# Four conditioning vectors of the attention layer: from TensorE steps to scaled sums on GpSimd and ScalarE

## The chip, the cores and the metric

The kernel runs on one core of one Trainium2 chip. The time is the device time of one execution in microseconds (us). The engines are named as in the profile: PE is TensorE's matmuls and PEld its weight loads, DVE is VectorE, ACT ScalarE, POOL GpSimd, SP SyncE; a "q" behind a name (SPq) is the part of an engine that issues transfers.

## What is computed

A backbone of two layers on 512 latent tokens and 256 context tokens of width 1024. Layer 0 mixes tokens by a Fourier transform and a short convolution, layer 1 by windowed attention with 16 query heads and 4 key heads; each layer ends in a mixture of 32 experts. Every layer has six conditioning vectors per sample, made by one product with a large matrix:

```python
mod_l = (silu(c) @ w_mod[layer] + b_mod[layer])[:, None, :]     # c: (1, 1024), w_mod[layer]: (1024, 6144)
mod_c = silu(c_ctx) @ w_mod[layer] + b_mod[layer]
sh1_l, sc1_l, g1_l, sh2_l, sc2_l, g2_l = split(mod_l, 6, axis=-1)
hl = modulate(rms_norm(xl, norm_mix_g[layer]), sh1_l, sc1_l)
...
yl, yc = window_attention(hl, hc, ...)                          # layer 1: softmax(q k + sink) v, then @ w_o
xl = xl + g1_l * yl
hl2 = modulate(rms_norm(xl, norm_ffn_g[layer]), sh2_l, sc2_l)
xl = xl + g2_l * hier_moe(hl2, ...)                             # last layer: latent tokens alone
```

In layer 1, the last, the context's part of the last four vectors (gate g1, shift sh2, scale sc2, gate g2) is not needed.

## The kernel before

**Conditioning.** A `ModFeed` makes two vectors (a group, 2048 columns) in four steps. A step has 2 MB of `w_mod` (two of the eight slices of 128 rows, 2048 columns) in a shared slot and multiplies it by `sil`, the silu of both samples, on TensorE: 8 matmuls of 512 columns at line 1035, recorded as 16. In layer 1, for groups 1 and 2 (g1 to g2), VectorE adds each step's PSUM tile to `bm` (line 1040), where GpSimd's queue has put `b_mod` (line 1028); after a group's four steps GpSimd's queue stores the rows of `bm` to `mod_d` in memory (line 1043). SyncE loads the weights (line 1013). Of these eight steps two stand in the projection of Q, K and V and six behind attention blocks 1 to 6.

**Attention** works on eight blocks (two halves of the heads by four blocks of 128 queries). Round `n` of the loop computes the scores and the exponentials of block `n`, two heads in each of four parts `i` (score matmul line 1783; mask and maximum on VectorE, line 1787; exponential with its sum on ScalarE, line 1789), and turns the probabilities of block `n-1` into values: `pv_tile` transposes eight heads' probabilities on TensorE (line 1830) and copies them out of PSUM (line 1833; tiles of the second four heads with odd `t` on VectorE, all others on ScalarE), `pv_mm` multiplies by V into the one PSUM tile `O` (line 1845). `s_end` works out the reciprocal of the softmax denominator in `es` (lines 1810 to 1813). `pv_end` spreads it over the partitions by TensorE (line 1856), and scales: ScalarE copies the factors (1858), VectorE multiplies them with `O` into SBUF (1859), ScalarE rounds the result to `ohi` (1862), VectorE takes the rest, `olo` (1863).

**Projection by w_o** (`mixer_out`): the matrix comes in two halves of 512 columns, hf0 in slot 2 and hf1 in slot 1, by four transfers each of 64 partitions (line 1893). For each of eight row slices ScalarE rounds it (line 1344) and VectorE takes the rest (line 1345); a tile of 128 tokens takes 24 matmuls (line 1378). `router` loads two vectors as `md` (line 1325) and has 8 matmuls with it (line 1331) within the first token tile of hf0. Behind hf1 the experts' weights (line 721) stream through a ring of buffers, among them the two that hold the rounded w_o.

**Order.** The code is written in the order of the loops; a scheduler then fixes each engine's order ahead of time. Every engine, SyncE's queue of transfers among them, works through its own list in order, so an instruction that waits holds all behind it. The buffers of a pool decide when a transfer may start: slot 1 holds the copied probabilities (`av`), slot 2 the conditioning weights.

Of the kernel before, what the change touches and what calls it, by code (L numbers as in the profile page):

```python
# [10 lines left out]
F32 = mybir.dt.float32  # L11
# [3 lines left out]
AF = mybir.ActivationFunctionType  # L15
# [5 lines left out]
D = 1024  # L21
# [64 lines left out]
def body(tc, I, out, upto=None, dbg=None):  # L86
# [57 lines left out]
    ones = one_.to_broadcast([128, 128])  # L144
    epst = stat.tile([128, 1], F32, name="epst")
    V.memset(epst, EPS)
    rsq = stat.tile([128, 2, 4], F32, name="rsq")

    def slot(i, shape, dt=F32):
# [22 lines left out]
    def rows_and_logits(m, xm, hq, a2, b2, ws, crow, route, h2dst, wk, psum):  # L172

        xv = xm.rearrange("t (p k) -> t k p", k=8)
        parts, last = isinstance(h2dst, list), m == route.NT - 1
        h2 = hq.tile([128, D], F32, name="h2", bufs=2 if parts else 3)
        ss = small.tile([128, 1], F32, name="ss")
        if last:

            s0 = small.tile([128, 1], F32, name="s0")  # L180
            r0 = small.tile([128, 1], F32, name="rb")
            S.activation(h2[:, 0:512], xm[:, 0:512], AF.Square, accum_out=s0)
            V.tensor_scalar(r0, s0, 1.0 / D, EPS, op0=ALU.mult, op1=ALU.add)
            if not parts:
                G.tensor_mul(h2[:, 0:512], xm[:, 0:512], a2[:, 0:512])
            yield
        hT = wk.tile([128, 8, 128], F32, name="hT")
        for hf in range(2):
            p = psum([128, 4, 128])
            for q in range(4):  # L190
                T.transpose(p[:, q, :], xv[:, hf * 4 + q, :], ident)
            S.copy(hT[:, hf * 4:hf * 4 + 4, :], p)
        if last:
# [803 lines left out]
    class ModFeed:  # L997
# [20 lines left out]
        def step(self, again=-1):  # L1018
# [22 lines left out]
            if q == 3:  # L1041
                for s in range(2):
                    G.dma_start(mod_d[l, s, g * 2048:(g + 1) * 2048].rearrange("(q n) -> q n", q=4), bm[s:128:32, :])


    xsrc = [I["x"][0, m * 128:(m + 1) * 128, :] for m in range(4)] + [I["ctx"][0, m * 128:(m + 1) * 128, :] for m in range(2)]
    pp = pool("ps0", space=PSUM)
# [535 lines left out]
    run(rest0)  # L1583

    feed = ModFeed([(1, 1), (1, 2)], lambda: cps([128, 512]), False)
    feed.load(0)
    close(mps, R1b, R1a, mp)
    pp = pool("ps1", space=PSUM)  # L1590
    kvp = pool("kvp")
# [3 lines left out]
    gqk = ro.tile([128, 2, 64], F32, name="gqk")  # L1595
    with tc.issue_after(near["done"].ins):
        rotary()
    cb = pool("cb")
    hpl = pool("hpl", side="right")

# [102 lines left out]
            S.copy(kS[part][0:64, :, ms], p)  # L1703
            (V.tensor_copy)(kS[part][64:128, :, ms], p)

    feed.psum_tile = lambda: psB([128, 512])
    raw0 = load_qkv(0, 3)
    for i in range(8):
        if i == 4:
            hc = slot(0, [128, 2, 8, LC], F32R)  # L1710
            hhi.append(hc[:, 0])
            hlo.append(hc[:, 1])
        for f, d in ((st_norm, 0), (st_kv, 1), (st_kt, 3)):
            if 0 <= i - d < (4 if f is st_kt else 6):
                f(i - d)
        if i == 0:
            feed.step()
        if i == 2:
            feed.step(None)
    close(cb)  # L1720

    qS = []
# [79 lines left out]

    ohi, olo = [hpl.tile([128, 8, L], F32R, name=n) for n in ("hhi", "hlo")]
    av = slot(1, [128, 8, 512])
    feed.load(2)
    def s_end(n):
        G_ = n // 4
        nm, ls = st_[n][1:3]
        es = small.tile([128, 8], F32, name="es")
        V.tensor_add(es, nm, sink[:, G_ * 8:G_ * 8 + 8])  # L1810
        S.activation(es, es, AF.Exp)
        V.tensor_add(es, es, ls)
        V.reciprocal(es, es)
        st_[n][3] = pp.tile([128, 512], F32, name="O", bufs=1)
        st_[n][4] = es

    pts = [0]

    def pv_tile(n, t):
        G_, b = divmod(n, 4)  # L1820
        Ps, po = st_[n][0], st_[n][3]
        kt = blk(b)[0]
        nk = len(kt)
        if t >= nk:
            return
        pt = []
        for gl in range(2):
            p = psB([128, 4, 128])
            for i in range(4):
                T.transpose(p[:, i, :], Ps[gl * 4 + i][:, t * 128:(t + 1) * 128], ident)  # L1830
            d = av[:, pts[0] % 4]
            pts[0] += 1
            (V.tensor_copy if gl and t % 2 else S.copy)(d, p.rearrange("p i q -> p (i q)"))  # L1833
            pt.append(d)
        st_[n].append(pt)

# [11 lines left out]
    def pv_end(n):  # L1848

        G_, b = divmod(n, 4)  # L1850
        po, es = st_[n][3:5]
        p = psB([128, 4, 128])
        for i in range(4):
            for gl in range(2):
                c = gl * 4 + i
                T.matmul(p[gl * 64:gl * 64 + 64, i, :], es[:, c:c + 1].to_broadcast([128, 64]), ident, start=True, stop=True)
        o = av[:, 4 + n % 2]
        S.copy(o, p.rearrange("p i q -> p (i q)"))
        V.tensor_mul(o, o, po)
        ov = o.rearrange("p (i q) -> p i q", i=4)  # L1860
        hs = ohi[:, G_ * 4:G_ * 4 + 4, b * 128:(b + 1) * 128]
        S.copy(hs, ov)
        V.tensor_sub(olo[:, G_ * 4:G_ * 4 + 4, b * 128:(b + 1) * 128], ov, hs.bitcast(F32))

    s_end(0)
    for n in range(1, 9):
        if n < 8:
            s_begin(n)
        for i in range(5):
            if n < 8 and i < 4:  # L1870
                s_head(n, 2 * i)
                s_head(n, 2 * i + 1)
            if n == 1 and i < 2:
                st_qt(1, 2 + i)
            if n > 0:
                pv_tile(n - 1, i)
                pv_mm(n - 1, i - 1)
        if n > 0:
            pv_mm(n - 1, 4)
            pv_end(n - 1)  # L1880
        if n < 7:
            feed.step()
        if n < 8:
            s_end(n)
    close(wp, ro, ap_, kvp, fdp)

    wov = I["w_o"][0].rearrange("(G gl i d) n -> gl d G i n", G=2, gl=2, i=4)

# [69 lines left out]
```

## Time and profile before

| | |
|---|---|
| time, median of 3 runs (lowest, highest) | 1679.38 us (1678.43, 1681.98) |
| profiled execution: its time, its span | 1680.04 us, 1678.1 us |
| busy: PE, DVE, ACT, POOL | 1557.0, 726.6, 441.8, 124.5 us |
| mean granted clock of TensorE, share of full | 0.967 |
| read from memory, mean rate | 499.31 MB, 301 GB/s |

The span runs from the first to the last instruction of one execution. The busy times are sums over stages with different limits, so a stage is read from its own stretch. Rows name a line of the kernel, an engine, an operation, and `out<-in` by the program's names; what stands in brackets at a row's end is how long the engine was idle just before, and what ended that.

### The profile page before, as it was taken

How to read it: one execution, taken by the hardware profiler on the slowest of the kernel's cores; microseconds unless marked ns; L12 is line 12 of the kernel's file. 1: busy time of each engine (PE TensorE's matmuls, PEld its weight loads, DVE VectorE, ACT ScalarE, POOL GpSimd, SP SyncE). 2: the span in 40 equal slices, each digit the busy share in tenths (PEclk: the TensorE clock that was granted, in tenths of full speed). 3: DMA queues.
4: the chain of work that ended last, by engine and by line, in shares of the span. 5: the costliest groups of instructions: out<-in, count | busy, mean ns of one | idle time of the engine just before them, and what ended most of it. 6: DMA issues, size and time to landing. Idle time of an engine off the chain costs nothing.

```text
span 1678.1 us, 21585 instructions
## 1 busy us (share of the span) xinstructions
PE 1557.0 (93%) x8123; PEld 869.8 (52%) x8123; DVE 726.6 (43%) x1638; ACT 441.8 (26%) x879; POOL 124.5 (7%) x128
## 2 busy tenths in 40 slices
PE   5999989889999999999889999999899999986787
PEld 3677878634444444444357765558444544531332
DVE  4432335963325443434468954545622322320213
ACT  5321212211111111111256665544221221210110
POOL 2510001300000000000212300000000000000000
PEclk8999989889999999999989999999899999999899
DMA  9775253789999999999811114253699999999996
GB/s 375 273 283 191 86 195 101 273 329 419 420 419 402 384 419 419 420 419 420 338 71 51 49 56 186 75 140 75 263 420 420 419 420 420 419 418 421 420 420 253
DMA packets 106398, 503.52 MB, mean 300 GB/s; under 512 B 18384, under 2 KB 33232, under 8 KB 52272
## 3 DMA queue, kind: packets, MB, share of 16 engines
q1 hardware_dynamic: 95776, 464.09, 69.9%
q0 software_dynamic: 7344, 34.81, 5.4%
q10 hardware_dynamic: 3168, 3.17, 0.6%
q8 instruction: 67, 1.10, 0.3%
q14 instruction: 43, 0.35, 0.1%
HBM read 499.31 MB, written 5.34 MB: 301 GB/s over the span
## 4 chain that ended last, share of the span: by engine, by line
PE 35%; DMA 10%; DVE 3%; ACT 2%; issue 1%; SPq 0%; DVEq 0%; ACTq 0%
PE p L860 8%; DMA w<-in_w_dram 5%; PE yp L931 5%; DMA hhi<-in_w_dram 3%; PE cp L809 3%; PE O L1845 3%; PE A L1378 3%; PE tp L765 3%; PE A L1660 2%; PE B L1830 2%; PE A L1783 2%; PE B L1035 1%; DMA r<-in_w_dram 1%; PE tp L772 1%; DMA w<-in_w_qkv_dram 1%
## 5 line engine op out<-in xcount | busy, mean ns | idle before, releaser
L860 PE MATMUL p<-w,xt 128*64 128x512 f32 (+1 forms) x1024 | 336.5, 611 | 16.6 <-DMA w<-in_w_dram 16.5
L860 PE MATMUL p<-r,xt 128*64 128x512 f32 (+1 forms) x784 | 284.5, 614 | 11.5 <-DMA r<-in_w_dram 11.0
L810 DVE TENSOR_TENSOR x<-x,cp 128x512 f32<-128x512 f32 x224 | 148.0, 685 | 96.6 <-PE cp L809 96.5
L809 PE MATMUL cp<-y,ot 128*128 128x512 f32 x616 | 173.6, 417 | 10.7 <-DVE x L810 6.9
L873 DVE TENSOR_TENSOR sg<-sg,p 128x512 f32<-128x512 f32 x29 | 20.0, 688 | 369.8 <-PE p L860 358.4
L860 PEld LDWEIGHTS p<-w,xt 128*64 128x64 f32 (+1 forms) x1024 | 100.2, 134 | 129.7 <-issue 98.2
L931 PE MATMUL yp<-w,ht 128*64 128x512 f32 (+1 forms) x512 | 162.7, 602 | 2.9 <-DMA w<-in_w_dram 2.9
L860 PEld LDWEIGHTS p<-r,xt 128*64 128x64 f32 (+1 forms) x784 | 84.3, 137 | 146.4 <-issue 122.6
L809 PEld LDWEIGHTS cp<-y,ot 128*128 128x128 f32 x616 | 106.8, 191 | 53.9 <-DVE x L810 28.3
L931 PE MATMUL yp<-r,ht 128*64 128x512 f32 (+1 forms) x368 | 131.6, 613 | 2.1 <-DMA r<-in_w_dram 1.4
L797 ACT CAST y<-yp 128x512 fp32r<-128x512 f32 x58 | 34.0, 586 | 280.7 <-DVE yp L793 185.5
L1378 PE MATMUL A<-r,r 128*128 128x512 f32 x288 | 72.9, 411 | 2.6 <-ACT r L1344 2.4
L931 PEld LDWEIGHTS yp<-r,ht 128*64 128x64 f32 (+1 forms) x368 | 38.5, 137 | 67.8 <-issue 63.7
L931 PEld LDWEIGHTS yp<-w,ht 128*64 128x64 f32 (+1 forms) x512 | 47.0, 132 | 47.0 <-issue 39.5
L860 PE MATMUL p<-hhi,xt 128*64 128x512 f32 (+1 forms) x128 | 62.6, 642 | 6.6 <-DMA hhi<-in_w_dram 6.6
L1787 DVE CUSTOM_DVE_ANT_0 A<-A,band,nsink 128x640 f32<-128x640 f32 (+1 forms) x56 | 46.5, 833 | 47.4 <-PE A L1783 36.4
L1378 PEld LDWEIGHTS A<-r,r 128*128 128x128 f32 x288 | 56.1, 198 | 14.9 <-ACT r L1344 2.7
L863 ACT ACTIVATE sg<-p 128x512 f32<-128x512 f32 x29 | 17.3, 597 | 157.4 <-PE p L860 157.4
L799 DVE TENSOR_TENSOR y<-yp,y 128x512 fp32r<-128x512 f32 x58 | 40.1, 692 | 40.3 <-ACT y L797 40.3
L1845 PE MATMUL O<-w,v 128*64 128x512 f32 x144 | 56.9, 615 | 0.6 <-ACT w L1833 0.6
L795 DVE SCALAR_TENSOR_TENSOR yp<-yp,gs,grow 128x512 f32<-128x512 f32 x26 | 19.7, 759 | 77.7 <-PE yp L931 77.7
L860 PE MATMUL p<-hlo,xt 128*64 128x512 f32 (+1 forms) x112 | 52.5, 618 | 0.0
(428 smaller groups left out, 2560.7 us busy)
## 6 DMA issues: line engine op xcount, KB each, us to landing
w<-in_w_dram SPq DMA_DIRECT2D x191, 1024.0 KB, 19.8
r<-in_w_dram SPq DMA_DIRECT2D x143, 1024.0 KB, 19.8
w<-in_w_mod_dram POOLq DMA_DIRECT2D x12, 2048.0 KB, 8.6
hhi<-in_w_dram SPq DMA_DIRECT2D x23, 1024.0 KB, 19.7
hlo<-in_w_dram SPq DMA_DIRECT2D x23, 1024.0 KB, 19.8
w<-in_w_mod_dram SPq DMA_DIRECT2D x11, 2048.0 KB, 8.8
w<-in_w_in_even_dram SPq DMA_DIRECT2D x13, 512.0 KB, 9.0
w<-in_w_out_even_dram SPq DMA_DIRECT2D x2, 2048.0 KB, 8.2
```

Source lines behind the costliest of these rows:

```text
L765: T.matmul(p, oh[:, m, :], near["h2"][m][i][:, hf * 512:hf * 512 + 512], start=n == 0, stop=n == 7)
L797: hi = S.copy(Yr[j, hf][0], ys)
L799: V.tensor_sub(Yr[j, hf][1], ys, Yr[j, hf][0].bitcast(F32))
L809: T.matmul(p, OT[j][:, m * 128:(m + 1) * 128], Yr[j, hf][i], start=n == 0 and i == 0, stop=n == len(js) - 1 and i == 1)
L810: return V.tensor_add(xs, xs, p)
L860: T.matmul(ps[rs], X[b][:, q, rs], W[j, wn, ab][:, q, :], start=q == 0, stop=q == 7)
L931: T.matmul(py_[hf][rs, :], HT[b][:, q % 4, rs], W[j, "w2", ab][:, q % 4, hf * 512:hf * 512 + 512], start=q % 4 == 0, stop=q % 4 == 3)
L1378: T.matmul(ps, lhs(m, a, j), whl[b][:, j, :], start=j == 0 and i == 0, stop=j == 7 and i == 2)
L1660: T.matmul(ps, h[st][:, k, ms], whl[k][b], start=k == 0 and i == 0, stop=k == 7 and i == 2)
L1783: T.matmul(ps[:, o0:o0 + w], qS[G_][:, c, b * 128:(b + 1) * 128], kS[part][:, 2 * G_ + c // 4, k0:k0 + w], start=part == 0, stop=part == 1)
L1787: V.tensor_tensor_reduce(out=ps[:, 0:w], in0=ps[:, 0:w], in1=bnd, op0=ALU.add, op1=ALU.min, scale=1.0, scalar=nsink[:, hd:hd + 1], accum_o ...
L1845: T.matmul(po[gl * 64:gl * 64 + 64, :], vts[kt[t]][:, (2 * G_ + gl) * 64:(2 * G_ + gl) * 64 + 64], pt[gl], start=t == 0, stop=t == nk - 1)
```

## The change

Vectors 2 to 5 of layer 1 are now made by a `SumFeed`, 16 steps of 1 MB (one vector, two row slices). In a step GpSimd multiplies the first slice by its 128 values of `sil` and ScalarE the second, and GpSimd adds them to a running sum of 128x1024. When the four steps of a vector are done, `finish` sums over the partitions by two matmuls with ones, VectorE adds `b_mod`, and SyncE stores the row. Only the latent sample is computed. The steps stand within the blocks, after parts `i` of rounds 1 to 7; finishes at the start of rounds 4, 6 and 7 and behind round 8. Slot 2 is cut in two rooms of 1 MB. With it: the two small additions of `s_end` go to GpSimd (`s_sum`, at part 2 of the next round), all copies for the second four heads go to VectorE, and `pv_end` multiplies within PSUM, so that `ohi` and `olo` are read from there.

```diff
+        def load(self):
+            if self.ld < len(self.todo):
+                v, q = self.todo[self.ld]
+                c = self.vectors[v] * D
+                Y.dma_start(self.room[self.ld % len(self.room)], I["w_mod"][self.layer].rearrange("(p k) n -> p k n", k=8)[:, 2 * q:2 * q + 2, c:c + D])
+                self.ld += 1
+
+        def step(self):
+            v, q = self.todo[self.cp]
+            w, acc = self.room[self.cp % len(self.room)], self.acc[v % 2]
+            self.cp += 1
+            for i in range(2):
+                t = w[:, i] if q + i else acc
+                if i:
+                    S.activation(t, w[:, i], AF.Copy, scale=sil[:, 2 * q + i, 0:1])
+                else:
+                    G.tensor_scalar(t, w[:, i], sil[:, 2 * q + i, 0:1], None, op0=ALU.mult)
+                if q + i:
+                    G.tensor_add(acc, acc, t)
+            self.load()
+
+        def finish(self, ps):
...
+            rows = bm[0:64:32, :]
+            Y.dma_start(rows, I["b_mod"][self.layer, c:c + D].rearrange("(q n) -> q n", q=2))
+            for cb in range(2):
+                T.matmul(ps[cb * 32:cb * 32 + 32, :], onef.to_broadcast([128, 32]), acc[:, cb * 512:cb * 512 + 512], start=True, stop=True)
+            V.tensor_add(bm[0:64], ps[0:64], bm[0:64])
+            Y.dma_start(mod_d[self.layer, 0, c:c + D].rearrange("(q n) -> q n", q=2), rows)
...
-        if i == 0:
-            feed.step()
-        if i == 2:
-            feed.step(None)
...
-    feed.load(2)
+    wm = slot(2, [128, 2, 2, D])
+    feed = SumFeed(1, (2, 3, 4, 5), [wm[:, 0], wm[:, 1]], acc)
...
+        G.tensor_add(es, nm, sink[:, G_ * 8:G_ * 8 + 8])
         S.activation(es, es, AF.Exp)
-        V.tensor_add(es, es, ls)
+        G.tensor_add(es, es, ls)
...
-            (V.tensor_copy if gl and t % 2 else S.copy)(d, p.rearrange("p i q -> p (i q)"))
+            (V.tensor_copy if gl else S.copy)(d, p.rearrange("p i q -> p (i q)"))
...
-        V.tensor_mul(o, o, po)
-        ov = o.rearrange("p (i q) -> p i q", i=4)
+        V.tensor_mul(po, po, o)
+        ov = po.rearrange("p (i q) -> p i q", i=4)
...
+            if i == 2:
+                s_sum(n - 1)
+            if i == 0 and n in (4, 6, 7):
+                feed.finish(psB([128, 512]))
+            if i in {1: (0, 2, 4), 4: (0, 2, 4), 8: ()}.get(n, (1, 3)):
+                feed.step()
...
+        if n == 8:
+            feed.finish(psB([128, 512]))
```

The lines of before that the text names move by some 40: the scores 1783 to 1822, the values 1845 to 1888, the rounding of w_o 1344 to 1389, its matmuls 1378 to 1423, its loads 1893 to 1940. New are 1061 (load), 1071 and 1073 (scaling on ScalarE and GpSimd), 1075 (addition), 1084 to 1088 (finish).

SyncE's list at the end of attention, before: `w_8410` is hf0 of w_o (slot 2), `w_8557` hf1 (slot 1), `w_8938` and `w_8939` experts' weights, `wr` to `gf` the router's.

```order
L1893 DMA w_8410<-in_w_o_dram 64x4x512 x4
L721 DMA w_8938<-in_w_dram 128x2048 x2
L1314 DMA wr<-in_w_router_g_dram 128x8x4
L1315 DMA wr<-in_w_router_e_dram 128x8x32
L1316 DMA br<-in_b_router_g_dram 128x4
L1317 DMA br<-in_b_router_e_dram 128x32
L1319 DMA gf<-in_norm_ffn_g_dram 128x8
L1337 DMA gr<-mod_d 128x512
L1325 DMA md_8433<-mod_d 128x2x8
L1337 DMA gr<-mod_d 128x512
L721 DMA w_8939<-in_w_dram 128x2048
L1893 DMA w_8557<-in_w_o_dram 64x4x512 x4
```

The same place now: `w_7074` is the sixteenth load of the conditioning weights, `w_8413` hf0 of w_o, `w_8560` hf1. The two halves of an expert's weights (here `w_8939`) stand just ahead of these rows.

```order
L1359 DMA wr<-in_w_router_g_dram 128x8x4
L1061 DMA w_7074<-in_w_mod_dram 128x2x1024
L1360 DMA wr<-in_w_router_e_dram 128x8x32
L1361 DMA br<-in_b_router_g_dram 128x4
L1362 DMA br<-in_b_router_e_dram 128x32
L1364 DMA gf<-in_norm_ffn_g_dram 128x8
L1382 DMA gr<-mod_d 128x512
L1940 DMA w_8560<-in_w_o_dram 64x4x512 x4
L1382 DMA gr<-mod_d 128x512
L1940 DMA w_8413<-in_w_o_dram 64x4x512 x4
L1088 DMA mod_d<-bm 2x512
L1370 DMA md_8436<-mod_d 128x2x8
```

The loads of hf0 have moved from ahead of the experts' weights to behind those of hf1, and the load of `md` behind them; the last load of the conditioning weights stands behind the router's first.

TensorE's list at the same place, before, from the last value matmuls into the projection (`r_8400` is the rounded w_o, `r_8401` its rest). The router's matmuls (line 1331) follow after 16 matmuls of line 1378.

```order
L1845 MATMUL O<-w_7094,v_5925 64x512 x2
L1856 MATMUL B<-cst,es 64x128 x8
L1845 MATMUL O<-w_7094,v_5926 64x512 x2
L1378 MATMUL A<-r_8400,hhi 128x512
L1378 MATMUL A<-r_8400,hlo 128x512
L1378 MATMUL A<-r_8400,hhi 128x512
L1378 MATMUL A<-r_8400,hlo 128x512
L1378 MATMUL A<-r_8401,hhi 128x512
```

The same place now (`acc_5913` is the running sum of the fourth vector, `r_8403` the rounded w_o).

```order
L1888 MATMUL O<-w_7073,v_5928 64x512 x2
L1899 MATMUL B<-cst,es 64x128 x8
L1888 MATMUL O<-w_7073,v_5929 64x512 x2
L1086 MATMUL B<-acc_5913,onef 32x512 x2
L1423 MATMUL A<-r_8403,hhi 128x512
L1423 MATMUL A<-r_8403,hlo 128x512
L1423 MATMUL A<-r_8403,hhi 128x512
L1423 MATMUL A<-r_8403,hlo 128x512
L1376 MATMUL B<-wr,md_8436 128x36 x8
```

The two matmuls of the last finish now stand between the last values and the projection, and the router's matmuls after 4 of the projection's matmuls instead of 16.

## Rows read from the trace of the kernel before

**Rows 1.** windows: busy us of PE, PEld, DVE, ACT, POOL, then granted clock, DMA share, GB/s
```profile
920.00:940.00 20.00, 19.08 (x96) 15.18 (x96) 19.12 (x43) 8.17 (x18) 6.56 (x5) 1.00 0.00 0
980.00:1000.00 20.00, 20.00 (x128) 11.29 (x124) 9.13 (x20) 10.60 (x23) 0.00 (x0) 1.00 0.28 106
```

**Rows 2.** groups of instructions in attention: count, busy us, mean ns, idle before
```profile
L1833 ACT COPY w<-B 128x512 f32<-128x512 f32 x56 | 32.6, 588 | 33.7 <-PE B L1830 30.0 <-PE O L1845 3.3
...
L1035 PE MATMUL B<-w,sil 128*32 128x512 f32 x96 | 16.1, 601 | 0.0
...
L1833 DVE COPY w<-B 128x512 f32<-128x512 f32 x16 | 11.0, 689 | 13.9 <-PE B L1830 13.9
```

**Rows 3.** timeline of TensorE around three feed steps: start, duration, name
```profile
854.35 3.60 PE L1035 MATMUL B<-w,sil 128*32 128x512 f32 x16 [2.67 <-ACT r L1556]
857.88 2.12 PE L1660 MATMUL A<-w,hhi 128*128 128x512 f32 x8
...
870.01 1.92 PE L1035 MATMUL B<-w,sil 128*32 128x512 f32 x16
871.87 1.16 PE L1552 MATMUL B<-cst,xn 128*128 128x128 f32 x8
...
1021.15 1.05 PE L1035 MATMUL B<-w,sil 128*32 128x512 f32 x4
1022.13 0.74 PE L1783 MATMUL A<-kS,w 128*128 128x256 f32 x4
```

**Rows 4.** two stretches at the first feed step, with the granted clock (PEclk)
```profile
856.00:858.00 2.00, 2.00 (x13) 0.32 (x6) 0.00 (x0) 1.83 (x6) 1.81 (x1) 0.56 0.00 0
858.00:860.00 2.00, 2.00 (x9) 1.64 (x10) 1.98 (x12) 0.00 (x0) 0.00 (x0) 1.00 0.53 94
```

**Rows 5.** GpSimd's groups: additions, scalings and casts
```profile
L201 POOL TENSOR_TENSOR h<-x,a 128x1024 f32<-128x1024 f32 x4 | 9.6, 2410 | 124.2 <-ACT h L199 124.2
...
L1148 POOL TENSOR_SCALAR xnl<-xnl,A,AB 128x512 f32<-128x512 f32 x3 | 3.3, 1106 | 0.0
...
L1515 POOL CAST w<-r 128x512 fp32r<-128x512 f32 x4 | 2.3, 604 | 0.0
```

**Rows 6.** ScalarE's operation on 128x1024
```profile
L1670 ACT ACTIVATE xn<-x,rq x4: 1134/1149/1152, 860.9 to 880.5; 128x1024 f32<-128x1024 f32 x4
```

**Rows 7.** SyncE's queue at the end of attention
```profile
1086.96 2.63 SPq L1893 DMA_DIRECT2D w<-in_w_o_dram  x4
1108.70 5.26 SPq L721 DMA_DIRECT2D w<-in_w_dram  x2
1114.06 0.58 SPq L1314 DMA_DIRECT2D wr<-in_w_router_g_dram  x1
```

**Rows 8.** timeline of TensorE from the last score matmul to the projection
```profile
1107.89 0.74 PE L1783 MATMUL A<-kS,w 128*128 128x256 f32 x4
...
1118.05 0.50 PE L1378 MATMUL A<-r,hhi 128*128 128x512 f32 x1 [0.34 <-ACT r L1344]
...
1119.99 0.62 PE L1378 MATMUL A<-r,hhi 128*128 128x512 f32 x2
...
1120.68 0.62 PE L1378 MATMUL A<-r,hhi 128*128 128x512 f32 x2
...
1123.89 1.94 PE L1331 MATMUL B<-wr,md 128*128 128x36 f32 x16 [1.67 <-issue]
```

**Rows 9.** the eight w_o loads, from issue to landing
```profile
DMA to landing us min/median/max: 5.7/8.5/11.2
```

**Rows 10.** DMA issues: count, KB each, median us to landing
```profile
r<-in_w_qkv_dram SPq DMA_DIRECT2D x2, 1024.0 KB, 6.8
...
md<-mod_d SPq DMA_DIRECT2D x3, 8.0 KB, 4.4
```

**Rows 11.** second w_o half's transfer, experts' stage: DMA share, GB/s
```profile
1132.00:1140.00 8.00, 8.00 (x37) 6.56 (x36) 2.57 (x4) 0.00 (x0) 0.00 (x0) 1.00 1.04 208
1300.00:1600.00 300.00, 269.02 (x1366) 116.28 (x1366) 74.07 (x120) 57.06 (x120) 0.00 (x0) 0.95 1.01 420
```

More of the change, by code (lines that the diff above doesn't have):

```diff
@@ L146, in body @@
     V.memset(epst, EPS)
+    onef = stat.tile([128, 1], F32, name="onef")
+    V.memset(onef, 1.0)
     rsq = stat.tile([128, 2, 4], F32, name="rsq")
@@ L178, in rows_and_logits @@
         if last:
-            s0 = small.tile([128, 1], F32, name="s0")
-            r0 = small.tile([128, 1], F32, name="rb")
+            s0, r0 = rsq[:, 0, 0:1], rsq[:, 0, 1:2]
             S.activation(h2[:, 0:512], xm[:, 0:512], AF.Square, accum_out=s0)
@@ L1043, in step, with __init__ @@
                     G.dma_start(mod_d[l, s, g * 2048:(g + 1) * 2048].rearrange("(q n) -> q n", q=4), bm[s:128:32, :])
+    class SumFeed:
+        def __init__(self, layer, vectors, room, acc):
+            self.layer, self.vectors, self.room, self.acc = layer, vectors, room, acc
+            self.todo = [(v, q) for v in range(len(vectors)) for q in range(4)]
+            self.ld = self.cp = self.out = 0
+            for _ in room:
+                self.load()
[17 more added lines that the diff above has]
+                    G.tensor_add(acc, acc, t)
+            self.load()
+        def finish(self, ps):
+            c, acc = self.vectors[self.out] * D, self.acc[self.out % 2]
+            self.out += 1
+            assert 4 * self.out <= self.cp <= 4 * self.out + 4
+            rows = bm[0:64:32, :]
[4 more added lines that the diff above has]
+            Y.dma_start(mod_d[self.layer, 0, c:c + D].rearrange("(q n) -> q n", q=2), rows)
     xsrc = [I["x"][0, m * 128:(m + 1) * 128, :] for m in range(4)] + [I["ctx"][0, m * 128:(m + 1) * 128, :] for m in range(2)]
@@ L1583, in body @@
     run(rest0)
-    feed = ModFeed([(1, 1), (1, 2)], lambda: cps([128, 512]), False)
-    feed.load(0)
     close(mps, R1b, R1a, mp)
@@ L1597, in body @@
         rotary()
+    accp = pool("accp")
+    acc = [accp.tile([128, D], F32, name=f"acc{i}") for i in range(2)]
     cb = pool("cb")
@@ L1704, in st_kt @@
             (V.tensor_copy)(kS[part][64:128, :, ms], p)
-    feed.psum_tile = lambda: psB([128, 512])
     raw0 = load_qkv(0, 3)
@@ L1804, in body, with s_sum @@
     av = slot(1, [128, 8, 512])
-    feed.load(2)
+    wm = slot(2, [128, 2, 2, D])
+    feed = SumFeed(1, (2, 3, 4, 5), [wm[:, 0], wm[:, 1]], acc)
     def s_end(n):
+        st_[n][3] = pp.tile([128, 512], F32, name="O", bufs=1)
+        st_[n][4] = small.tile([128, 8], F32, name="es")
+    def s_sum(n):
         G_ = n // 4
-        nm, ls = st_[n][1:3]
-        es = small.tile([128, 8], F32, name="es")
-        V.tensor_add(es, nm, sink[:, G_ * 8:G_ * 8 + 8])
+        nm, ls, es = st_[n][1], st_[n][2], st_[n][4]
+        G.tensor_add(es, nm, sink[:, G_ * 8:G_ * 8 + 8])
         S.activation(es, es, AF.Exp)
-        V.tensor_add(es, es, ls)
+        G.tensor_add(es, es, ls)
         V.reciprocal(es, es)
-        st_[n][3] = pp.tile([128, 512], F32, name="O", bufs=1)
-        st_[n][4] = es
     pts = [0]
@@ L1874, in body @@
                 st_qt(1, 2 + i)
[L1875 to L1882, printed above, removed]
+            pv_tile(n - 1, i)
+            pv_mm(n - 1, i - 1)
+            if i == 2:
[4 more added lines that the diff above has]
+                feed.step()
+        pv_mm(n - 1, 4)
+        pv_end(n - 1)
+        if n == 8:
+            feed.finish(psB([128, 512]))
         if n < 8:
             s_end(n)
-    close(wp, ro, ap_, kvp, fdp)
+    close(wp, accp, ro, ap_, kvp, fdp)
     wov = I["w_o"][0].rearrange("(G gl i d) n -> gl d G i n", G=2, gl=2, i=4)
```

## The prediction

> **What bounds the kernel now.** I read the busy times by stretch first. In the attention stage TensorE is busy 20.00 of 20 us at full clock, while VectorE has 9 and ScalarE 11 [rows 1]: work taken off TensorE there should come back as time. In the projection of Q, K and V, VectorE is at 19.12 of 20 instead [rows 1], so a TensorE step less may come back only in part. Then the timeline at the end of attention [rows 7, 8]: TensorE passes from the last value matmul to the w_o projection with a wait of 0.34 us, because the first half of w_o (hf0) was issued at 1086.96, some 30 us ahead. Behind w_o the experts' weights stream at 420 GB/s with the DMA engines at 1.01 [rows 11], and their buffers come free with the projection's end; so whatever delays that projection delays the end of the kernel one for one.
>
> **The sum is made against the profiled execution**, 1680.04 us; the median shown is 0.66 lower.
>
> **Projection stage, -3.8.** Two feed steps go. The second fills 870.01 to 871.87, 1.86 us [rows 3]. The first fills 854.35 to 857.88, 3.5 us, because it runs at a granted clock of 0.56, that is mostly the 1.2 GHz level, after an idle TensorE; the 2.4 GHz level is back at 858 [rows 3, 4]. Without it other matmuls stand there, at half clock. Eight of L1660 take 2.12 us at full clock, about 1.9 without overlap [rows 3]; they fit into those 3.5 us at half clock, so 1.9 is saved and the rest is still paid. 1.86 + 1.9 = 3.8. Bounds: 5.4 (both whole) and 0 (VectorE's chain keeps the end, as its 19.12 allows).
>
> **Attention, -4.7.** Six steps of 1.86 go (the 96 records of [rows 2] are six times 16): -11.2. Three of the four finishes add two matmuls each; four such records fill 1021.15 to 1022.13, 0.98 us [rows 3], so +2.9. The remaining engines: 20 of 72 copies of transposed probabilities go from ScalarE (588 ns) to VectorE (689 ns) [rows 2], so 13.8 us more on VectorE. Taking off the two 8-column additions per block, the six bias additions (of the copies' length) and adding four for the finishes leaves about 10. ScalarE gets 16 scalings at 1.15 [rows 6] less 20 copies, +6.6. Spread over 150 us both have room, but a scaling of 1.15 ahead of a copy, and the one O bank held until the second VectorE operation of a block's end instead of the first (about 1.3 us longer, ScalarE's cast and VectorE's subtraction), make short waits. I take 0.5 us for each of the seven block boundaries, +3.5. So -11.2 + 2.9 + 3.5 = -4.7. Bounds: -8.2 (no wait) and +1 (1.3 us at each boundary).
>
> **End of attention, +22.** Here the diff says little and the order much. I count from L, the end of the last score matmul, 1108.6 [rows 8]. TensorE reached the projection at L+9.4 and, with 96 matmuls at three in 0.69 us, 16 router matmul records of 1.94 and the 1.67 wait ahead of them [rows 8], ended hf0 at about L+35.
> - SyncE issues the sixteenth 1 MB load only behind the expert's two halves and the router's first load. Before, the two halves took 5.26 us from L+0.1 (the second waits for the first to land) and the router load went at L+5.4 [rows 7]. So the last w_mod load goes at L+6. 1 MB lands after 5 us (that wait) to 6.8 [rows 7, 10]; I take 6, with the expert's half still ahead of it: L+12.
> - GpSimd then scales 128x1024: not in the trace; twice the 604 ns cast of 512 columns is 1.2, twice the 1106 ns of a two-scalar operation is 2.2 [rows 5]. I take 1.5, nearer the cast, since it is one scalar. Two additions of 2.41 [rows 5] follow: L+18.3.
> - The room of those weights, slot 2, is where hf0 now goes. Its four loads sit on SyncE behind the four of hf1, which wait only for the last attention block and, the third, for the sixteenth load. So 2 MB that are needed second go first. w_o loads move 208 GB/s while the DMA engines show 1.04 [rows 11]: 10 us for 2.1 MB, L+12 to L+22. A 512 KB piece alone lands in 5.7 [rows 9], 2.5 of it transfer. hf0's third piece, with which a first 128-row slice is whole, lands at L+29.7, its fourth at L+32.2.
> - TensorE waits for GpSimd in the last finish, then for that piece and ScalarE's cast: L+30.3 instead of L+9.4.
> - After four matmuls it comes to the router, which needs md; md's load stands behind hf0's fourth piece. Issued alone it lands in 4.4 [rows 10]; here just behind that piece, about L+33. Then 92 matmuls (21.2) and 1.94: L+56.3. The clock has dropped in the idle 20 us; the 854.35 row against the 870.01 row prices that at 1.7 [rows 3]: L+58, 23 later than before. I take 22, since md may be quicker.
>
> Bounds: hf0 issued at L+17.3 and arriving with nothing ahead of it (third piece 1.3 + 5.7 later, md not late, clock not lost) gives hf0's end at L+49, +14; a 2.2 us scaling, a landing of 6.8 and md 2 us later, +26.
>
> The Trainium skill's page "SBUF — State Buffer", section "Door 1: The DMA port swizzle (why `[64,N]` ≈ `[32,N]`)", has the reason for the slow loads: 64 partitions in one half of the memory reach 8 of 16 ports, for which it states 196 GB/s at 1 MiB and about 218 at most. By its figures hf1's 2.1 MB would take 9.6 to 10.7 us. The 208 GB/s of [rows 11] agree.
>
> **Hidden.** The 16 loads (one of 1 MB in every 10 us) and the early b_mod and mod_d transfers lie beside TensorE's work; the DMA engines have room there. GpSimd has 28 additions of 2.41 and 16 scalings of 1.5, 91 us in 150, on an engine that was nearly idle. If it fell behind, its small additions for the softmax denominators would be late, then the reciprocal, then the block's end.
>
> **Sum:** 1680.04 - 3.8 - 4.7 + 22 = 1693.5; less 0.66, **1693 us**, +0.8%.
>
> **Rivals.**
> - *The weights come at full rate, so not slower.* hf1's first two pieces go to the lower 64 partitions, the last two to the upper; if the DMA engines carried both halves at once, at the 420 GB/s of the experts [rows 11], hf1 would be in by L+17 and hf0's third piece by about L+23, with its end near L+48: a tail of 13. With the attention stage at its no-wait bound the sum is 1679.4 - 3.8 - 8.2 + 13 = 1680.4. It decides where hf0's third piece lands by about L+25. Against it: 208 GB/s with the engines full.
> - *GpSimd becomes the bound.* The eight blocks take the 160 us to 1118, 20 each. In the two with three steps GpSimd needs 3 x (1.5 + 4.8) = 19 of them. If VectorE's greater use of the memory stretches each addition by 40%, it is 25, 5 too late in each; with 2 us caught up behind its two buffers these blocks lose 8 together, and the chain behind the sixteenth load 2: 1703. For it: GpSimd has no such run of additions in the trace. Against: the other blocks have two steps, 13 us, and leave room.
> - *The removed TensorE work does not come back*, because copies on VectorE and the scalings on ScalarE now hold TensorE in both stages: 1679.4 + 22 = 1701. For it: 19.12 of 20 in [rows 1]; against: attention's 9 of 20.
> - *The change does not take its work off TensorE's path*, since the finishes still stand in its order and wait for GpSimd: at three of them the sums they need are done a block or more earlier, so nothing is lost there; the fourth is the tail above.
>
> The same page, section "Who interferes with whom", speaks for the second rival: a VectorE instruction with two SBUF inputs and a GpSimd instruction that reads SBUF exclude each other. No row here has enough of both to show it; by that rule the sum would move toward 1703.
>
> **How the numbers follow.** Forecast 0.62 (its own range 1686 to 1700), full rate 0.12, GpSimd 0.09, no return 0.10, and 0.07 for a smaller tail than any of my bounds. The lower end 1681 takes in most of the full-rate case; the upper, 1702, the no-return case. A measurement here tells about 0.2%, 3.4 us, from no change: below 1676 is faster, above 1682.7 slower. Faster: the 0.07 less a little, 0.05. Same: the full-rate case and a little, 0.13. Slower 0.82.
>
> **What the changed profile would show.** TensorE still near 20 of 20 in attention, with the block time shorter by about 0.7; an idle TensorE of about 20 us at the end of attention, first until GpSimd's last addition (L+18), then until the w_o pieces, put down to ScalarE's cast or the DMA; a second wait of 2 to 3 us ahead of the router; hf1's pieces landing before hf0's; a low granted clock behind the wait; the experts' stage as long as before. Wrong if the idle time is under 10 us, if GpSimd's additions take much more than 2.41, or if attention's span does not shrink.

## The result and the profile after

The changed kernel takes 1694.12 us (median of 6 runs, 1688.07 to 1695.27) against 1680.07 of the kernel before on the same chip (6 runs, 1678.16 to 1682.73): a ratio of 1.0073, 95% interval 1.0056 to 1.0089. It is slower by about 14 us. The profiled execution has a span of 1692.2 us, 14.1 more than that of before.

Stages apart, by the first and the last matmuls of each in the two traces. Attention is counted from the first score matmul of block 1, since block 0's scores are worked out within the projection; E is the end of the last value matmul, 1117.7 before and 1106.55 after.

| from, to | before, us | after, us | difference | forecast |
|---|---|---|---|---|
| start, first matmul of layer 1's projection | 854.35 | 849.84 | -4.5 | 0 |
| that, first score matmul of block 1 | 104.4 | 102.2 | -2.2 | -3.8 |
| that, E | 158.9 | 154.5 | -4.4 | -4.7 |
| E, first matmul with w_o | 0.35 | 22.7 | +22.4 | +22, all of the end |
| that, start of the last matmul with w_o (1172.2, 1187.3) | 54.1 | 58.05 | +3.9 | |
| that, end | 505.9 | 504.9 | -1.0 | 0 |

A second trace of the kernel before (e0_before_again, below) has 852.39, 104.0, 158.9, 0.34, 57.6 and 506.0 us in these rows. Against it the first row's difference is -2.6 and that of the row of +3.9 is +0.5; the others hardly move.

The two stretches that answer to [rows 1], in the same columns:

```profile
920.00:940.00 20.00, 20.00 (x104) 16.60 (x103) 18.70 (x43) 9.77 (x17) 6.50 (x5) 1.00 0.00 1
980.00:1000.00 20.00, 19.41 (x142) 13.59 (x138) 11.51 (x24) 12.99 (x27) 14.93 (x7) 1.00 0.32 106
```

TensorE still fills these stretches, GpSimd is now busy 15 of 20 us in attention, and VectorE and ScalarE have each got 2 more. Then the end of attention, TensorE's timeline (it answers to [rows 8]):

```profile
1105.52 1.03 PE L1888 MATMUL O<-w,v 128*64 128x512 f32 x4
1116.05 1.92 PE L1086 MATMUL B<-acc,onef 128*32 128x512 f32 x4 [9.49 <-POOL acc L1075]
1129.25 0.79 PE L1423 MATMUL A<-r,hhi 128*128 128x512 f32 x1 [11.28 <-ACT r L1389]
...
1131.33 3.60 PE L1376 MATMUL B<-wr,md 128*128 128x36 f32 x16
1134.74 1.20 PE L1423 MATMUL A<-r,hhi 128*128 128x512 f32 x2
```

TensorE idles 9.49 us until GpSimd's last addition, does the two matmuls of the last finish, idles 11.28 us until ScalarE has rounded a slice of w_o, and then has the router after four matmuls. ScalarE's rounding itself waits for the transfers of w_o:

```profile
1128.58 2.18 ACT L1389 CAST r<-w 128x512 fp32r<-128x512 f32 x4 [19.12 <-DMA w<-in_w_o_dram]
```

GpSimd's own timeline of that time:

```profile
1075.08 4.67 POOL L1075 TENSOR_TENSOR acc<-acc,w 128x1024 f32<-128x1024 f32 x2
...
1093.63 2.84 POOL L1073 TENSOR_SCALAR w<-w,sil 128x1024 f32<-128x1024 f32 x1 [3.07 <-DMA w<-in_w_mod_dram]
...
1098.91 7.27 POOL L1075 TENSOR_TENSOR acc<-acc,w 128x1024 f32<-128x1024 f32 x3
1108.31 2.84 POOL L1073 TENSOR_SCALAR w<-w,sil 128x1024 f32<-128x1024 f32 x1 [2.13 <-DMA w<-in_w_mod_dram]
1111.24 4.75 POOL L1075 TENSOR_TENSOR acc<-acc,w 128x1024 f32<-128x1024 f32 x2
```

The last three additions ahead of the final step keep it until 1106.2, it waits 2.13 us for the sixteenth load, scales for 2.84 and adds twice, to 1115.99. SyncE's queue beside it (as [rows 7]):

```profile
1087.81 0.48 SPq L1088 DMA_DIRECT2D mod_d<-bm  x1
1088.38 0.37 SPq L1061 DMA_DIRECT2D w<-in_w_mod_dram  x1
1089.06 0.34 SPq L722 DMA_DIRECT2D w<-in_w_dram  x1
...
1096.27 0.34 SPq L722 DMA_DIRECT2D w<-in_w_dram  x1
1101.43 0.60 SPq L1359 DMA_DIRECT2D wr<-in_w_router_g_dram  x1
1102.14 0.59 SPq L1061 DMA_DIRECT2D w<-in_w_mod_dram  x1
...
1107.42 2.65 SPq L1940 DMA_DIRECT2D w<-in_w_o_dram  x4
...
1116.02 2.58 SPq L1940 DMA_DIRECT2D w<-in_w_o_dram  x4
...
1119.35 0.37 SPq L1370 DMA_DIRECT2D md<-mod_d  x1
```

The order is as it was read: the two halves of an expert's weights (the second 7.2 us behind the first), the router's first load at 1101.43, the sixteenth load at 1102.14, hf1 at 1107.42, and hf0 only at 1116.02, when GpSimd is done.

The first rows of both views show where GpSimd lost time ahead of that. It ended the additions of step 13 (of the 16) at 1079.75, so the room of the fifteenth load was free. But that load stands behind the store of the third finish on SyncE's list, and went with it, at 1088.38. GpSimd has the scaling of that load ahead of the additions of step 14 on its own list, and stood idle for 10.7 of the 13.9 us up to 1093.63: 7.6 for the small additions of the softmax denominators, which stand ahead on its list and wait for ScalarE and VectorE, and 3.07 for this load. So step 14 ended at 1101.3, and only then was the room of the sixteenth load free. That load thus did not wait for the expert's halves: its room came free at 1101.3, and the router's first load ahead of it went at 1101.43.

Windows behind that, with the granted clock and the rate of the transfers at the end of the line (as [rows 11]):

```profile
1118.00:1126.00 8.00, 0.00 (x0) 0.00 (x0) 0.68 (x1) 0.00 (x0) 0.00 (x0) 0.50 1.07 220
1129.00:1140.00 11.00, 10.74 (x32) 8.71 (x33) 5.55 (x11) 3.93 (x8) 0.00 (x0) 0.50 0.34 105
1140.00:1150.00 10.00, 10.00 (x43) 8.07 (x42) 2.78 (x4) 0.00 (x0) 0.00 (x0) 0.98 0.33 107
```

hf1 and hf0 come at 220 GB/s with the DMA engines at 1.07, as slow as before. TensorE, idle for 20 us but for two matmuls, starts again at a granted clock of 0.50, the 1.2 GHz level, and gets the 2.4 GHz level back only at about 1140.

GpSimd's two large groups in the change (count, busy us, mean ns, idle before):

```profile
L1075 POOL TENSOR_TENSOR acc<-acc,w 128x1024 f32<-128x1024 f32 x28 | 66.8, 2387 | 0.9
L1073 POOL TENSOR_SCALAR w<-w,sil 128x1024 f32<-128x1024 f32 x12 | 34.1, 2840 | 9.8 <-DMA w<-in_w_mod_dram 9.8
```

An addition takes 2.39 us, as it did in [rows 5], but a scaling takes 2.84, longer than the addition of two operands.

### The profile page after: what moved, and what is told of

Same layout as the page of the kernel before. It is cut to its first block, busy times and chain, and to the rows that moved or that the text cites. A ratio compares the mean times of both kernels' runs of the same rounds, so it can differ in the third digit from the quotient of the medians.

```text
span 1692.2 us, 21472 instructions
## 1 busy us (share of the span) xinstructions
PE 1538.8 (91%) x8011; PEld 871.4 (51%) x8011; DVE 730.3 (43%) x1639; ACT 448.6 (27%) x875; POOL 234.4 (14%) x180
## 4 chain that ended last, share of the span: by engine, by line
PE 34%; DMA 11%; DVE 3%; ACT 2%; issue 1%; POOL 0%; SPq 0%; ACTq 0%; DVEq 0%; POOLq 0%
PE p L861 8%; PE yp L932 5%; DMA w<-in_w_dram 5%; DMA hhi<-in_w_dram 4%; PE A L1704 3%; PE cp L810 3%; PE A L1423 3%; PE O L1888 2%; PE tp L766 2%; PE B L1873 2%; PE A L1822 2%; DMA w<-in_w_mod_dram 1%; DMA w<-in_w_o_dram 1%; PE tp L773 0%; DMA w<-in_w_qkv_dram 0%
## 5 line engine op out<-in xcount | busy, mean ns | idle before, releaser
L738 POOL DMA_INDIRECT r<-h_d,gi x17 | 16.9, 996 | 414.2 <-PE tp L773 345.5
L1075 POOL TENSOR_TENSOR acc<-acc,w 128x1024 f32<-128x1024 f32 x28 | 66.8, 2387 | 0.9
L1423 PE MATMUL A<-r,hhi 128*128 128x512 f32 x128 | 44.4, 422 | 11.3 <-ACT r L1389 11.3
## 6 DMA issues: line engine op xcount, KB each, us to landing
w<-in_w_mod_dram SPq DMA_DIRECT2D x3, 2048.0 KB, 10.7
```

Source lines behind the costliest of these rows:

```text
L1075: G.tensor_add(acc, acc, t)
L1423: T.matmul(ps, lhs(m, a, j), whl[b][:, j, :], start=j == 0 and i == 0, stop=j == 7 and i == 2)
```

## The experiments

Each compares with the kernel before on the same chip and gives its ratio with the 95% interval. The first group asks what the tail, the time lost between E and the end of the projection by w_o, is made of.

**e1_hf0_first**: the two halves of w_o trade slots.

```diff
-                      lambda hf: load_wo(hf, 1 if hf else 2), ...
+                      lambda hf: load_wo(hf, 2 if hf else 1), ...
```

> The two halves of w_o trade slots: hf0 goes to slot 1, hf1 to slot 2, so SyncE issues hf0 ahead of hf1 and hf0 waits only for the last attention block. E is the end of the last value matmul. My theory (2 MB needed second stand ahead of hf0, and hf0 waits for GpSimd): the first projection matmul comes at about E+11.5, right behind the last finish, instead of E+22.8; the router then waits for md, which now stands behind hf1, until about E+20.5 instead of E+24.9, so the whole gains 4 us: 1690. Rival (the transfers are late whatever their order, the DMA engines are the limit): first projection matmul at E+20 or later and 1694.

1691.71 us, 1.0076 (1.0051 to 1.0102), so no gain that can be told from the change's 1.0073. TensorE and SyncE at the end of attention (E is 1103.3 here):

```profile
1102.25 1.03 PE L1888 MATMUL O<-w,v 128*64 128x512 f32 x4
1112.41 1.92 PE L1086 MATMUL B<-acc,onef 128*32 128x512 f32 x4 [9.14 <-POOL acc L1075]
1115.49 0.80 PE L1423 MATMUL A<-r,hhi 128*128 128x512 f32 x1 [1.16 <-ACT r L1389]
...
1128.42 3.60 PE L1376 MATMUL B<-wr,md 128*128 128x36 f32 x16 [10.86 <-DMA md<-mod_d]
```

```profile
1104.14 2.65 SPq L1940 DMA_DIRECT2D w<-in_w_o_dram  x4
...
1112.39 2.58 SPq L1940 DMA_DIRECT2D w<-in_w_o_dram  x4
...
1115.72 0.37 SPq L1370 DMA_DIRECT2D md<-mod_d  x1
```

The first matmul with w_o did come at E+12.2 instead of E+22.7, as the order theory says, and not at E+20. But the router then waited 10.86 us for md, issued at 1115.72 behind hf1's four loads and landed at E+25: 5 us later than I had written, and hardly earlier than in the change. The delay goes with the order on SyncE's queue; taking the right half first only hands the wait to the next load in the line. The last matmul with w_o lies 81.0 us behind E here, 80.8 in the change.

**e4_actscale**: ScalarE scales both slices, GpSimd only adds.

```diff
-                if i:
-                    S.activation(t, w[:, i], AF.Copy, scale=sil[:, 2 * q + i, 0:1])
-                else:
-                    G.tensor_scalar(t, w[:, i], sil[:, 2 * q + i, 0:1], None, op0=ALU.mult)
+                S.activation(t, w[:, i], AF.Copy, scale=sil[:, 2 * q + i, 0:1])
```

> Both slices of a step are scaled by ScalarE, GpSimd only adds (28 x 2.39 = 67 us instead of 112). In the order hf0 now stands ahead of the last expert's weights again. My theory (the tail is the chain: sixteenth load, scaling 2.84 and two additions on GpSimd, then hf0): the last addition comes some 8 us before E, hf0 is in by E+3, TensorE idles less than 4 us there, and the tail of 26 shrinks to 4 or less; ScalarE's 18 us more cost 3 to 6 in attention: 1676, range 1671 to 1682. Rival (the tail is the w_o transfers at 208 GB/s): at least 10 us of idle TensorE remain, 1686 or more.

1670.07 us, 0.9943 (0.9925 to 0.9962): by the two ratios 22 us less than the change, and faster than the kernel before. It is just under the range written down: ScalarE's 18 us more cost attention nothing (first score matmul to E: 153.5 us, the change 154.5). GpSimd's last additions, hf0's issue, and TensorE's first matmul with w_o:

```profile
1070.56 4.86 POOL L1072 TENSOR_TENSOR acc<-acc,w 128x1024 f32<-128x1024 f32 x2 [1.34 <-ACT w L1070]
```

```profile
1076.01 2.67 SPq L1937 DMA_DIRECT2D w<-in_w_o_dram  x4
```

```profile
1106.26 0.50 PE L1420 MATMUL A<-r,hhi 128*128 128x512 f32 x1 [2.00 <-ACT r L1386]
```

GpSimd is done at 1075.4, not 8 but 29 us before E, and hf0 goes at 1076.0. TensorE waits 2.00 us at the end, for ScalarE's rounding. From the first matmul with w_o to the last it takes 55.7 us, between the 54.1 and 57.6 of the two traces of before.

**e10_dvescale**: VectorE instead of GpSimd for the first slice, ScalarE as in the change.

```diff
-                    G.tensor_scalar(t, w[:, i], sil[:, 2 * q + i, 0:1], None, op0=ALU.mult)
+                    V.tensor_scalar(t, w[:, i], sil[:, 2 * q + i, 0:1], None, op0=ALU.mult)
```

> The change with VectorE instead of GpSimd for the first slice's scaling; ScalarE keeps the second. If only GpSimd's 2.84 us per scaling makes the feed late: the tail goes as in e4_actscale (hf0 ahead of the last expert's weights in the order), and the time is 1668 to 1674. A scaling of 128x1024 on VectorE is not in any trace; if it takes 1.4 us (twice a copy of 512 columns), VectorE has 22 us more and attention loses 0 to 4 against e4_actscale, whose ScalarE has 18 us more; rival (VectorE blocks GpSimd's additions or the maxima): over 1676.

1668.62 us, 0.9932 (0.9912 to 0.9951). The scaling on VectorE (ns of one: least, median, most):

```profile
L1073 DVE TENSOR_SCALAR w<-w,sil x12: 745/749/2010, 963.9 to 1071.0; 128x1024 f32<-128x1024 f32 x12
```

0.75 us against 2.84 on GpSimd for the same 128x1024. GpSimd's additions stay at a mean of 2.39. It is VectorE that waits: three of its sixteen scalings take 1.12 to 2.01 us, and each of them began during a GpSimd addition and ended 0.55 us behind the addition's end. This one word takes the whole tail away, so GpSimd's scaling is its cause. How it acts is not taken apart: with the scaling the scheduler's lists changed too, and the third finish's store now stands behind the sixteenth load (1077.53 against 1065.93). No run changed the lists alone, so how much of the tail comes from GpSimd's 2.84 us and how much from the lists is open.

**e5_six_blocks** and **e5b_six_blocks_pool**: the sixteen steps in rounds 1 to 6, the first with both scalings on ScalarE, the second scaled as in the change.

```diff
-            if i == 0 and n in (4, 6, 7):
+            if (n, i) in ((3, 0), (4, 0), (6, 0), (7, 4)):
                 feed.finish(psB([128, 512]))
-            if i in {1: (0, 2, 4), 4: (0, 2, 4), 8: ()}.get(n, (1, 3)):
+            if i in {5: (1, 3), 6: (1, 3), 7: (), 8: ()}.get(n, (0, 2, 4)):
...
-        if n == 8:
-            feed.finish(psB([128, 512]))
```

> As e4_actscale, and the 16 steps are done in rounds 1 to 6 (three each in 1 to 4), finishes in rounds 3, 4, 6 and 7. My theory: slot 2 is free a block and more before E, hf0 is there in time, TensorE goes into the projection with less than 1 us of wait as in the kernel before; ScalarE has 6.9 us more in each of four blocks of 18: 1675, range 1669 to 1682. Rival (removed TensorE work does not come back, ScalarE and VectorE hold attention): no tail but 1680 or more.

> Steps and finishes as in e5_six_blocks, but scaled by GpSimd and ScalarE in turn as in the change. GpSimd has 16 x 7.0 = 112 us and more for 110 us of blocks. If GpSimd is the bound of the feed (theory, from its 2.84 us for a scaling): its additions run over into round 7, the softmax denominators that stand behind them come late and hold the ends of blocks, attention is 5 or more longer than in e5_six_blocks, but the tail is under 8: 1682, range 1676 to 1690. Rival (GpSimd has room): the same time as e5_six_blocks within 3 us.

1676.49 us, 0.9981 (0.9967 to 0.9995), and 1685.10 us, 1.0031 (1.0017 to 1.0045). Both lie in the ranges written down, and neither has a tail (the first matmul with w_o comes 0.9 and 1.2 us behind the last value matmul's start). From the first score matmul to that last value matmul's start they take 158.0 and 165.5 us, e4_actscale 152.9, the change 153.9, the kernel before 158.3. So with denser steps attention gives back what the steps saved on TensorE (5 us between e4_actscale and e5), and with GpSimd's scalings it loses 7 more. Where, shows TensorE's timeline of e5b:

```profile
1037.61 1.92 PE L1086 MATMUL B<-acc,onef 128*32 128x512 f32 x4 [3.38 <-POOL acc L1075]
...
1105.07 1.92 PE L1086 MATMUL B<-acc,onef 128*32 128x512 f32 x4 [5.06 <-POOL acc L1075]
```

Two finishes wait for GpSimd's sums, 3.38 and 5.06 us, where e5 has no such wait. In this form the rival with GpSimd as the bound is true.

The second group asks what attention itself lost. In the change, ScalarE at its start:

```profile
954.00 1.28 ACT L160 ACT_TABLE_LOAD   x1
...
957.08 1.15 ACT L1071 ACTIVATE w<-w,sil 128x1024 f32<-128x1024 f32 x1 [1.49 <-DMA w<-in_w_mod_dram]
958.25 1.28 ACT L1828 ACT_TABLE_LOAD   x1
959.54 0.69 ACT L1828 ACTIVATE P<-B,nm 128x512 f32<-128x512 f32 x1
```

TensorE, and the granted clock:

```profile
955.78 0.92 PE L1822 MATMUL A<-kS,w 128*128 128x256 f32 x6 [1.02 <-DVE sq L1688]
960.38 1.97 PE L1783 MATMUL B<-cst,x 128*128 128x128 f32 x8 [3.68 <-ACT P L1828]
```

```profile
955.00:960.00 5.00, 0.92 (x6) 0.77 (x6) 4.14 (x15) 3.47 (x5) 4.13 (x3) 0.96 0.75 302
960.00:965.00 5.00, 4.62 (x22) 4.63 (x23) 2.15 (x4) 5.00 (x13) 5.00 (x3) 0.50 0.00 0
```

Between its change of tables for the root and that for the exponentials ScalarE waits 1.49 us for the first load and scales for 1.15; TensorE, which waits for the exponentials, idles 3.68 us and then runs at 0.50, the 1.2 GHz level. The end of block 1 (the first of the matmuls that spread the denominators, line 1899) comes 26.1 us after the first score matmul, before 19.4.

**e9_late_start** moved the first steps to later parts of the loop on top of e4_actscale (`{1: (2, 4), 2: (0, 2, 4), 4: (0, 2, 4), 8: ()}`).

> e4_actscale with one step moved from round 1 to round 2 and round 1's two steps later (parts 2 and 4), so that no scaling stands on ScalarE's list between its change of tables and the first exponentials of attention. My theory (in the change and in e4_actscale ScalarE waits there for the first load and scales while TensorE has nothing to do, 3.7 us, and the clock then falls to half for 4 us): block 1's end comes 3 to 6 us earlier counted from the first score matmul, the time falls by 3 to 5 to 1666. Rival (the lead is lost to something else, or lost again in the next blocks): block 1's end as in e4_actscale or the time within 1.5 us of it.

1669.70 us, 0.9940 (0.9920 to 0.9960), block 1's end at 26.0. The forecast missed, but this tells nothing about the theory: the place in the loop does not set the place on ScalarE's list, and the first scalings still stood between the two tables.

**e11_after_exp** puts an edge there, on top of e10_dvescale.

```diff
+                if feed.cp:
+                    feed.step()
+                else:
+                    with tc.issue_after(last0.ins):
+                        feed.step()
```

(`last0` is the last exponential of block 0.)

> e10_dvescale, with the first step's instructions ordered behind the last exponential of block 0, so that ScalarE's first scaling no longer stands between its change of tables and the exponentials (e9_late_start was meant to do this, but its list kept the scaling there). My theory (ScalarE's wait for the first load of 1.5 us and the scaling of 1.15 hold TensorE 3.7 us at the start of attention, and the half clock behind it costs as much again): the first idle time falls to about 1 us, block 1's end comes 4 to 6 us earlier counted from the first score matmul (20 to 21 instead of 25.3), and the time falls by 3 to 5, to 1664 to 1666. Rival (the blocks behind it are held by VectorE and ScalarE anyway, the lead is lost again): block 1's end earlier, but the end of attention and the time within 1.5 us of e10_dvescale.

1672.19 us, 0.9945 (0.9928 to 0.9963), on a chip where the kernel before took 1681.12; e10_dvescale had 0.9932, so there is no gain. TensorE at the start of attention:

```profile
956.70 1.32 PE L1783 MATMUL B<-cst,x 128*128 128x128 f32 x8 [1.05 <-ACT P L1828]
...
962.25 1.54 PE L1822 MATMUL A<-kS,w 128*128 128x256 f32 x6 [2.06 <-ACT P L1828]
```

The 3.73 us of idle TensorE that e10_dvescale has there have become 1.05 and 2.06, and block 1 ends at 23.3 instead of 25.4. But the end of attention lies 155.6 us behind the first score matmul, in e10_dvescale 153.7 (both to the last value matmul's start): as the rival has it, the lead is lost again in the blocks behind. My theory for this idle time fell: it is there, but in this kernel it costs nothing by the end of attention.

**e8_copies_back** (on the change) and **e12_copies** (on e11_after_exp) undo the moved copies.

```diff
-            (V.tensor_copy if gl else S.copy)(d, p.rearrange("p i q -> p (i q)"))
+            (V.tensor_copy if gl and t % 2 else S.copy)(d, p.rearrange("p i q -> p (i q)"))
```

> The change with the copies of transposed probabilities split as before (VectorE only those of the second four heads with odd t): 20 copies of 0.59 go back to ScalarE, 13.8 us leave VectorE. My theory (the waits in attention are ScalarE's: scalings stand ahead of exponentials): slower by 1 to 5 us than the change, 1695 to 1699, with more idle TensorE put down to exponentials. Rival (VectorE's share made the waits): faster, 1691 or less.

> e11_after_exp with the copies of transposed probabilities split as before (VectorE only those of the second four heads with odd t). VectorE has taken 12 us of scalings here and gives back 13.8 us of copies, ScalarE takes 11.8. If VectorE is now what TensorE waits for in attention: faster than e11_after_exp by 1 to 4 us; if ScalarE is (theory): slower by 1 to 4; within 1.5 us: neither, the choice of engine for these copies does not matter here.

1692.44 us, 1.0080 (1.0060 to 1.0100) against the change's 1.0073, and 1673.57 us, 0.9955 (0.9938 to 0.9973) against 0.9945. Neither difference can be told from none; the traces give attention 1.7 us less and 2.8 us more. So neither theory of e8 came out, and no effect of the choice of engine for these twenty copies is seen.

**e0_before_again** is the kernel before once more.

> The kernel before, once more, for a second trace: in the change and in all four runs so far layer 1 starts (first matmul of the projection) at 847.5 to 850.2 us, against 854.35 for the first feed step in the trace of before. If that lead comes with the change, the feed step starts at 853 to 856 again; if executions differ by as much, it starts at 852 or earlier.

Its feed step starts at 852.39, between the two cases written down; in the ten traces of the change and its variants layer 1 starts at 847.3 to 851.4. So part of the 4.5 us that appeared ahead of layer 1 is scatter between executions. 1.3 us of it stand in every trace: the mixer of layer 0 runs through in 69.7 us (last feed matmul to first matmul of its output projection) in all ten traces of the change and its variants, and in 71.0 in both traces of before. Its TensorE list is the same there. What causes it, and whether more than these 1.3 us come with the change, is open.

This trace shows scatter in the projection by w_o too, without any change to the kernel:

```profile
1121.74 3.50 PE L1331 MATMUL B<-wr,md 128*128 128x36 f32 x16 [1.92 <-issue]
```

```profile
1121.85:1128.67 6.82, 6.82 (x25) 6.05 (x26) 3.59 (x7) 0.00 (x0) 0.00 (x0) 0.50 0.44 142
```

Here the granted clock falls to 0.50 at the router, behind a wait of 1.92 us, and the projection takes 57.6 us. In the first trace of before it does not fall behind 1.67 us [rows 8], and the projection takes 54.1.

## Why the prediction was right

The time, 1693 forecast and 1694.1 measured, and the place were right: the wait at the end of attention, for GpSimd and then for hf0. That the time agrees to 1 us is luck, since several terms were off and cancel. Attention as a whole, from the first score matmul of block 1 to E, before and after, in the columns of [rows 1]:

```profile
958.77:1117.70 158.93, 154.78 (x979) 90.94 (x977) 81.99 (x193) 91.19 (x208) 4.80 (x7) 1.00 0.36 120
952.03:1106.55 154.52, 141.58 (x895) 90.97 (x893) 90.18 (x194) 96.22 (x202) 108.25 (x58) 0.96 0.39 136
```

The parts, in the order of the forecast's steps:

- **Projection stage, -3.8: measured -2.2** (-1.8 against the second trace of before). Over-sized by 1.6. In the variants' traces it is -2.1 to -3.1; VectorE was named as the reason why a part may not come back, and was not tried.
- **Attention, -4.7: measured -4.4.** The sum was right, two of its terms were not, and they cancel. TensorE's busy time fell by 13.2 us where the forecast has 8.3 (11.2 less 2.9), and its idle time rose by 8.8 (from 4.1 to 12.9, span less busy time) where it has 3.5. The first comes mostly from the price of a step: 1.86 us was taken from a step in the projection, while [rows 2] has 16.1 us for the 96 records in attention, 2.7 a step. As for the second, the waits do not lie at the block boundaries, 0.5 us each. 10.0 of the 12.9 us are waits for ScalarE's exponentials; in the largest, 3.68 us at the start, a scaling stands ahead of them, and behind it the clock falls. e11 showed, on top of e10, that shortening this one does not shorten attention, which leaves the chain of copies and exponentials through all blocks as what sets the end; that is argued, not shown, and how much each engine adds to it stays open. e5 shows that a denser feed costs all 4 us of the gain.
- **End of attention, +22: measured +26.3**, or +22.9 against the second trace of before; 22.4 of it is up to the first matmul with w_o. Counted from E, the times of the chain were near: sixteenth load at E-4.4 (forecast E-3.1, when L is taken at E-9.1), in at E+1.7 (E+2.9), last addition at E+9.4 (E+9.2), first matmul with w_o at E+22.7 (E+21.2), router at E+24.8 (E+23.9). Two links were mis-sized and cancelled in part: GpSimd's scaling was taken at 1.5, with 2.2 as the bound, and takes 2.84; the load landed earlier. The first link was right by luck. The last score matmul, from which I counted, lies 17.5 us before E in the change instead of 9, since the order of scores and values moved too, and the sixteenth load went at L+13 instead of L+6. What held it was not the expert's halves but its room, free when GpSimd had ended step 14 at 1101.3, and the router's first load, which waited for transposes on TensorE that ended at 1101.36; that GpSimd itself is late the forecast had as a rival and not as a link. The term that was short is the clock: 1.7 was taken from a step after 2.67 us of idle time [rows 3]; after 20 us TensorE ran at 0.50 from 1129.25 to 1140, with the router at 3.60 us instead of 1.94. If half the clock costs nearly half of these 11 us, as the router's rows suggest, that is about 5.5 us, an estimate; the 1.67 us of wait ahead of the router, which the change no longer has, give some of it back.
- **Nothing was forecast ahead of layer 1**; 4.5 us less stood there in the two traces, and 2.6 against the second trace of before. Against the first trace it made up for the 4.3 us that the tail was longer than forecast. Part of both is scatter, as the second trace shows.

The rivals: w_o at full rate fell (220 GB/s at 1.07). The Trainium skill's page "SBUF — State Buffer", section "Door 1: The DMA port swizzle (why `[64,N]` ≈ `[32,N]`)", has about 218 GB/s as the most for 64 partitions in one half, and the trace agrees within 1%. GpSimd as the bound of attention is false for the change (its additions kept a mean of 2.39 us, and the finishes in the middle did not wait for them) and true in e5b, with more steps to a block; its scaling is the cause of the tail, by e4 and e10.

The Trainium skill's page "SBUF — State Buffer", section "Who interferes with whom", says that a VectorE instruction with two inputs in SBUF contends with a GpSimd instruction that reads SBUF. The trace agrees where there is such a pair. VectorE first, then GpSimd:

```profile
967.46 1.53 DVE L1694 TENSOR_TENSOR x<-x 128x512 f32<-128x512 f32 x1
```

```profile
966.07 2.37 POOL L1075 TENSOR_TENSOR acc<-acc,w 128x1024 f32<-128x1024 f32 x1
968.52 2.73 POOL L1075 TENSOR_TENSOR acc<-acc,w 128x1024 f32<-128x1024 f32 x1
```

VectorE's subtraction took 1.53 us instead of its usual 0.69 and ended 0.55 behind GpSimd's addition, and the next addition took 2.73. But behind 969 us no large VectorE operation of attention has both its inputs in SBUF (the maxima, the copies and the ends of blocks read PSUM), so the mean of the additions hardly tests this rule.

That the removed TensorE work does not come back was half true for the change: of the 13.2 us that TensorE was less busy in attention 4.4 came back.

Faster than both kernels is e10_dvescale, at 0.9932 of the kernel before.

## What to carry to other kernels

A feed that is moved to idle engines keeps its buffers for as long as the slowest of these engines needs, and what is loaded next into the same buffers inherits that; read from the order which load will wait for the last instruction of the feed, and what stands ahead of it on the queue. Take such a chain from its last free event link by link, with the nearest rows for each; it gave the place here, and the size with errors that cancelled, where busy shares (GpSimd at 14%) gave no hint. Start it early enough: here GpSimd stood idle for 10.7 us ahead of the link where the forecast began, by what stood ahead on its own list and on the queue. And try each simple operation on every engine that has room before the work is moved: one word, the scaling on VectorE, made a loss of 0.7% a gain of 0.7%.

## What was not expected of the hardware

A scaling of 128x1024 by one value per partition takes 2.84 us on GpSimd, 1.15 on ScalarE and 0.75 on VectorE; on GpSimd it is longer than an addition of two such operands (2.39), and 2.6 times a two-scalar operation on 128x512 (1106 ns, [rows 5]). A VectorE scaling that began during a GpSimd addition took up to 2.01 us. An idle TensorE of 20 us cost not only the wait: its next 11 us ran at the 1.2 GHz level. md, a load of 8 KB, landed 11.7 us after its issue behind four loads of w_o, where the median of the kernel before is 4.4 [rows 10].
